# conv_ffn: taps, silu and gate product on the products in PSUM, and GpSimd's share of the weight splits by a running sum

## The chip, the cores and the metric

One Trainium2 chip; the kernel runs on one of its cores. The metric is the device time of one execution in microseconds, the median of several runs. TensorE (PE) makes the matrix products into PSUM; VectorE (DVE), ScalarE (ACT) and GpSimd (POOL) work on tiles; SyncE (SP) issues the loads.

## The reference, cut to what matters

Two blocks of two layers each, all in float32, on 256 latent tokens and 256 context tokens of width 1024. The change bears on the feed-forward part at the end of each layer of the second block. It makes 2 x 2816 features of each token, convolves them over the tokens (the latents stand on a grid of 4 rows of 64 and get 3 x 3 taps; the context gets three taps along its row), and gates one half with the other:

```python
def conv_ffn(h, w_up, conv_w, conv_b, w_down, rows):
    u = h @ w_up
    if rows is None:
        u = dwconv1d(u, conv_w[1], conv_b)
    else:
        u = dwconv2d_grid(u, conv_w, conv_b, rows)
    a, g = jnp.split(u, 2, axis=-1)
    return (jax.nn.silu(g) * a) @ w_down
```

Layer 0 does this for latents and context, layer 1 for the latents alone.

## The kernel before

Every float32 product is made of three float32r products: each operand is the sum of a high and a low part, and `mm3` adds high times high, high times low and low times high. A weight is loaded into a `raw` tile (three of them, 1 MB each, `load`), and `wsplit` (line 413) makes `wh` on ACT, a copy of `raw`, and `wl`, the difference of `raw` and `wh`. That difference is made on DVE, or on GpSimd when the running number of splits is a multiple of `lo_pool`. `lo_pool` is set by stage: 4 or 5 in the first block and in the first mixer of the second, 2 in `conv_ffn` of layer 0, 3 in the mixer of layer 1, 1 in `conv_ffn` of layer 1, where GpSimd so makes every low half.

`conv_ffn` (line 1590) walks over 22 feature tiles of 128, two to a load. An iteration makes two products, of a tile of `a` and the tile of `g` that gates it (`q` 0 and 1), transposed: features on partitions, tokens along the row, 512 of them in layer 0 (`ns` 2: latents, then context) and 256 in layer 1. A product is eight times `mm3`, 24 matmuls. It lands in a PSUM tile of the tag `mm`, of which there are two. ACT reads it twice: `o` (tag `fo`, four tiles) is the middle tap with the bias, `u` (tag `fu`, three tiles) a copy in SBUF. The taps are then DVE instructions `o = u * w + o` (`stt`, line 187): eight for the latents, over 189, 192 or 252 of the 256 tokens, since the edges of the grid are left out, and in layer 0 two for the context, over 255. After both products of an iteration ACT takes silu of the second `o`, DVE multiplies the two `o`, ACT copies the result into the high half of `G` (named `cg` in the trace) and DVE subtracts to make the low half.

The down product (`dense_out`) uses `G` as its stationary operand, with three PSUM tiles `acc` and one `gv`; the two tiles of the tag `aux` serve transposes before and after `conv_ffn`. In layer 0 it runs after each of two parts (12 and 10 feature tiles). In layer 1 a group of its products, four feature tiles by both halves of the columns, is put after the feature tiles 8, 12, 16 and 20, a group behind, and the rest at the end. A scheduler at build time sets the order of each engine's queue from the dependences and the free tiles; on the chip each engine takes its queue in order.

Of the kernel before, what the change touches and what calls it, by code (L numbers as in the profile page):

```python
# [18 lines left out]
T = 256  # L19
# [10 lines left out]
# in each sub-block, the tiles of 128 columns to a step of the conditions' products  # L30
PACE = (6, 6.5, 8, 7, 7.5, 6.5)
# and the splits of weights to one whose low part is made by GpSimd
LO_POOL = (4, 4, 4, 4, 4, 5)
# the parts of the context's projections at the end of each sub-block of the first block
# [8 lines left out]
def _consts():  # L43
# [24 lines left out]
    # in both float32 and float32r  # L68
# [11 lines left out]
    # one-hot of the bucket of each distance j - 127  # L80
# [5 lines left out]
    # reversed, so that row p, column s reads p + s  # L86
# [8 lines left out]
    # name, reshape rows of 128  # L95
# [13 lines left out]
class _Pair:  # L109
    """hi and lo parts of a float32 tensor, each exact in float32r."""  # L110
# [11 lines left out]
class _K:  # L122
    def __init__(self, ctx, tc, I, out, dbg=None):
# [9 lines left out]
        self.nsplit = 0  # L133
# [9 lines left out]
    def fill(self, units):  # L143
        """one more step of the work for the gaps after each so many tiles of a matrix product"""
        self.credit += units
        while self.credit >= self.pace:
            self.credit -= self.pace
            next(self.filler, None)
# [5 lines left out]
    def weave(self, *gens):  # L154
        """traces (generator, steps) side by side, each at its share"""
        gens = [[g, n, 0] for g, n in gens]
        while gens:
            x = min(gens, key=lambda x: (x[2] + 0.5) / x[1])
            x[2] += 1
            try:  # L160
                next(x[0])
            except StopIteration:
                gens.remove(x)
# [34 lines left out]
    def silu2(self, out, p, th):  # L198
        """out = 2 silu(p); th: space for tanh"""
# [21 lines left out]
    def rows(self, pool, src, n, tag, bufs=1):  # L221
        """a vector of n in DRAM, the same in each partition"""
# [32 lines left out]
    def more_setup(self, pool):  # L255
        """what is wanted after the first products"""
# [17 lines left out]
    def all_mods(self):  # L274
        second = self.second_mods()
        for k in self.mods:
            if k == (1, 0):
                # the first norm's of the context are wanted early
# [6 lines left out]
    def vectors(self, b0, b1, raw, engs, loads=None):  # L285
        """vectors with the index along partitions: blocks b0 to b1 of 128 columns; raw [128, blocks, 128]"""
# [23 lines left out]
    def gemv(self, w, c0, conds):  # L310
        """partial sums [128, 512] of conds @ w[:, c0:c0+512], to be summed over partitions"""
# [15 lines left out]
    def gemv_cols(self, w, c0, conds, bias, outs, plus=0.0):  # L327
        """outs [128, 8]: cond @ w[:, c0:c0+1024] + bias + plus, by feature"""
# [10 lines left out]
    def start_loads(self):  # L339
        """the weights of the first modulation and the first rows"""  # L340
# [13 lines left out]
    def start_mod(self, A, B):  # L354
        """the first modulation, a part of it on the tensor engine"""
# [18 lines left out]
    def gemv_rows(self, w, c0, conds, bias, out, scale=1.0, plus=0.0):  # L374
        """out [conds, 1024] in DRAM: scale * (cond @ w[:, c0:c0+1024] + bias + plus); bias by feature"""
        n = len(conds)
        for h in range(2):
# [15 lines left out]
            # its product comes when its operand is there  # L393
# [19 lines left out]
    def wsplit(self, r):  # L413
        """[128, a, n], at most 1024 in a partition -> (hi, lo)"""
# [5 lines left out]
        self.nsplit += 1  # L420
        eng = self.nc.gpsimd if self.nsplit % self.lo_pool == 0 else None
# [3 lines left out]
    def mm3(self, out, stat, mov, start, stop):  # L425
        """out += stat.T @ mov, both (hi, lo)"""
# [7 lines left out]
    def prod_T(self, p, W, hT, ks=range(KT)):  # L434
        """p [n, T] = (h @ w).T for n columns of w"""
# [3 lines left out]
    def dense_T(self, hT, w, c0, n, evac, prep=None):  # L439
        """(h @ w[:, c0:c0+n]).T, evac(feature tile, psum [128, tokens])"""  # L440
# [11 lines left out]
    def dense_rows(self, hT, w, c0, n, evac, prep=None):  # L452
        """h @ w[:, c0:c0+n], evac(column, width, token tile, psum [128, width])"""
# [17 lines left out]
    def dense_out(self, stat, nk, w, evac, nt=2, both=False, tag="acc"):  # L471
        """g @ w with w [nk * 128, 1024]; stat(k): g.T's tile k as (hi, lo) [128, tokens]; evac(half, token tile,
        psum [128, 512]); both: the halves of the columns side by side up to the last tiles, else one after the other"""
        # the last ones' products are long, for what waits for the first tokens' results
# [27 lines left out]
    def to_T(self, n, A, B, hT, full=None):  # L502
        """n [128, 2, 1024] by tokens -> (n * A + B).T as a pair [128, 8, 256], and whole in full; A, B [128, 8]"""
# [25 lines left out]
    def ffn(self, hT, w_in, w_out, post, tail, more):  # L529
        """tail: what follows the last product; more: further work beside the first; both with room in the given pool"""  # L530
# [21 lines left out]
    def post_ln(self, i, x, Grow):  # L552
        """x: rows in DRAM; (evac of a dense_out, finish): LN(alpha x + G y) -> normalized rows, rows in DRAM"""
# [41 lines left out]
    def first_mod(self, l, j):  # L595
        """A = g (1 + scale), B = b (1 + scale) + shift, with the norm g, b before"""
# [13 lines left out]
    def first_block(self, n):  # L610
        """its first n sub-blocks"""
# [6 lines left out]
    def operand(self, i, hT=None):  # L618
        """the modulated rows ahead of sub-block i, by feature"""
# [3 lines left out]
    def sub_block(self, i, hT, nxt, before=None):  # L623
        """nxt: whether the next one's operand follows here; before: more to do ahead of the last product"""
# [16 lines left out]
        def tail(pool):  # L641
# [3 lines left out]
            # what the context's mLSTM needs, where the next products wait for the norm  # L645
# [22 lines left out]
    def mix_setup(self):  # L668
        nc, I = self.nc, self.I
        # rel_bias by distance: [128 queries, head, 256 keys], query 128 + q  # L670
# [21 lines left out]
    def lower_bound(self):  # L692
        nc, I = self.nc, self.I
        # 1 - lower bound of the second layer: softmax over layers, summed, less the first
# [47 lines left out]
    def merge(self, l, gp, YH, YL, sgd, post, more):  # L742
# [5 lines left out]
        for b in range(4):  # L748
# [6 lines left out]
            for i in range(2):  # L755
# [8 lines left out]
                # twice the sum; the half is in the gate  # L764
# [1172 lines left out]
```

## Time and profile before

| | |
|---|---|
| time, median of three runs | 3027.41 us (3025.47 to 3045.25) |
| span of the profiled execution | 3027.7 us |
| PE, DVE, ACT, POOL busy in the span | 89%, 80%, 44%, 28% |
| low halves made on GpSimd, on DVE | 233, 432 |
| taps of `conv_ffn` (DVE) | 792 |
| granted TensorE clock, mean | 0.948 |

The profile is that of one execution, which took as long as the median run. [...] "Idle before" is the time that an engine stood still ahead of a group of instructions, with what ended it. [...] The feed-forward part of layer 0 lies between about 1941 and 2318 us of the span, with two stretches of taps, and that of layer 1 between about 2720 and 3018 us.

### The profile page before, as it was taken

What the parts mean: (1) busy time and instruction counts of PE and PEld (TensorE: products, weight loads), DVE (VectorE), ACT (ScalarE), POOL (GpSimd) and SP (SyncE); (2) the same over time, 40 slices, a digit from 0 to 9 for tenths busy, and PEclk for the clock granted to TensorE, in tenths of its full rate; (3) what the DMA queues carried; (4) which work ended last, traced back from release to release, by engine and by line L of the source; (5) the groups of instructions that cost most, each with busy time, mean ns of one, the idle gap of its engine ahead of it and who ended that gap; (6) DMA issues with size and microseconds to landing.
All of it is one profiled execution on the core that took longest, in us unless ns stands there. A gap on an engine that the chain in (4) does not pass through costs nothing. (4 is left out here: it accounts for less than half of the span.)

```text
span 3027.7 us, 44224 instructions
## 1 busy us (share of the span) xinstructions
PE 2703.0 (89%) x16988; PEld 2398.9 (79%) x16988; DVE 2429.3 (80%) x3939; ACT 1337.1 (44%) x2171; POOL 834.3 (28%) x462
## 2 busy tenths in 40 slices
PE   7998998899899899989998998899988989886776
PEld 7987898799799788879987887777877767666665
DVE  7777898877888988797657767798596678879987
ACT  3444444444454444444445453543243534434433
POOL 1123121322321412232112212222222122425665
PEclk9998999899999999989999999999999999988888
DMA  9897677788798775678672141422322322233332
GB/s 317 277 316 245 216 231 245 225 293 273 237 310 287 227 243 185 207 235 298 228 217 85 32 143 51 162 84 98 98 74 90 89 67 71 83 111 99 112 112 97
DMA packets 406300, 534.78 MB, mean 177 GB/s; under 512 B 25061, under 2 KB 279881, under 8 KB 404553
## 3 DMA queue, kind: packets, MB, share of 16 engines
q1 hardware_dynamic: 404357, 531.22, 53.6%
q8 instruction: 133, 2.18, 0.3%
q10 hardware_dynamic: 1732, 0.74, 0.1%
q14 instruction: 78, 0.64, 0.1%
HBM read 515.61 MB, written 16.31 MB: 176 GB/s over the span
## 5 line engine op out<-in xcount | busy, mean ns | idle before, releaser
L175 POOL TENSOR_TENSOR wl<-raw,wh 128x1024 fp32r<-128x1024 f32 x233 | 619.0, 2662 | 1651.2 <-ACT wh L196 1472.9
L196 ACT ACTIVATE wh<-raw 128x1024 fp32r<-128x1024 f32 x665 | 696.1, 1053 | 761.5 <-PE mm L169 374.9
L169 PE MATMUL mm<-hTh,wh 128*128 128x256 f32 (+1 forms) x2552 | 805.6, 316 | 77.9 <-ACT fu L196 73.5
L169 PE MATMUL mm<-hTh,wl 128*128 128x256 f32 (+1 forms) x2552 | 791.6, 310 | 10.1 <-DVE wl L175 5.5
L169 PE MATMUL mm<-hTl,wh 128*128 128x256 f32 (+1 forms) x2552 | 793.1, 311 | 3.3 <-DVE hTl L175 3.3
L175 DVE TENSOR_TENSOR wl<-raw,wh 128x1024 fp32r<-128x1024 f32 (+1 forms) x432 | 537.0, 1247 | 193.2 <-ACT wh L196 190.6
L169 PEld LDWEIGHTS mm<-hTh,wh 128*128 128x128 f32 x2552 | 496.8, 195 | 115.7 <-ACT fu L196 83.8
L169 PEld LDWEIGHTS mm<-hTh,wl 128*128 128x128 f32 x2552 | 495.4, 194 | 34.6 <-DVE wl L175 6.4
L169 PEld LDWEIGHTS mm<-hTl,wh 128*128 128x128 f32 x2552 | 496.8, 195 | 27.4 <-DVE hTl L175 4.0
L187 DVE SCALAR_TENSOR_TENSOR fo<-fu,colv,fo 128x189 f32<-128x189 f32 (+3 forms) x792 | 468.0, 632 | 32.6 <-ACT fu L196 22.6
L187 DVE SCALAR_TENSOR_TENSOR acc<-graw,cond,acc 128x512 f32<-128x512 f32 x504 | 465.6, 939 | 23.6 <-ACT acc L196 9.6
L169 PE MATMUL acc<-wl,gh 128*128 128x512 f32 x352 | 139.4, 396 | 0.9 <-DVE wl L175 0.9
L169 PE MATMUL acc<-wh,cg 128*128 128x512 f32 x396 | 138.7, 409 | 1.6 <-ACT wh L196 1.6
L169 PE MATMUL acc<-wh,gh 128*128 128x512 f32 x352 | 140.0, 398 | 0.0
L169 PE MATMUL acc<-wh,gl 128*128 128x512 f32 x352 | 139.3, 396 | 0.0
L169 PE MATMUL mm<-hlh,wl 128*128 128x256 f32 (+1 forms) x456 | 130.9, 287 | 1.5 <-POOL wl L175 1.1
L169 PE MATMUL mm<-hll,wh 128*128 128x256 f32 (+1 forms) x456 | 130.4, 286 | 1.1 <-DVE hll L175 1.1
L169 PE MATMUL mm<-hlh,wh 128*128 128x256 f32 (+1 forms) x456 | 130.8, 287 | 0.3 <-DVE g L175 0.2
L169 PE MATMUL mm<-wh,hTh 128*128 128x256 f32 x384 | 114.3, 298 | 8.3 <-DVE hqT L187 3.6
L169 PE MATMUL mm<-wh,hTl 128*128 128x256 f32 x384 | 110.7, 291 | 2.5 <-DVE hTl L175 2.4
L169 PE MATMUL mm<-wl,hTh 128*128 128x256 f32 x384 | 111.4, 291 | 0.0
L196 ACT ACTIVATE fo<-fo 128x512 f32<-128x512 f32 (+1 forms) x44 | 23.1, 525 | 198.6 <-DVE fo L187 198.5
(546 smaller groups left out, 5142.7 us busy)
## 6 DMA issues: line engine op xcount, KB each, us to landing
raw<-in_ffn_w_in_dram SPq DMA_DIRECT2D x88, 1024.0 KB
graw<-in_w_ada_dram SPq DMA_DIRECT2D x128, 512.0 KB
raw<-in_mix_w_in_dram SPq DMA_DIRECT2D x52, 1024.0 KB
graw<-in_mod_w_dram SPq DMA_DIRECT2D x96, 512.0 KB
raw<-in_ffn_w_up_dram SPq DMA_DIRECT2D x44, 1024.0 KB
raw<-in_ffn_w_out_dram SPq DMA_DIRECT2D x40, 1024.0 KB
raw<-in_even_w_in_dram SPq DMA_DIRECT2D x28, 1024.0 KB
raw<-in_ffn_w_down_dram SPq DMA_DIRECT2D x20, 1024.0 KB
```

Of the source, the lines that this page charges most:

```text
L169: self.nc.tensor.matmul(out, lhsT, rhs, start=start, stop=stop)
L175: (eng or self.nc.vector).tensor_tensor(out=out, in0=a, in1=b, op=op)
L187: self.nc.vector.scalar_tensor_tensor(out, a, s, b, op0=op0, op1=op1, **kw)
L196: self.nc.scalar.activation(out, a, f, **kw)
```

## The change

Three edits, two of them in `conv_ffn`.

The copy `u` in SBUF is gone. The product's PSUM tile is itself `u`; it comes from the tags `mm` and `aux` in turn, two tiles each, so that products of `a` take one pair of banks and products of `g` the other. The taps read `u` there. Silu, which wrote over the second `o`, writes into the `u` of the second product, the gate product is written over it in PSUM, and the split of `G` reads it from there.

`wsplit` adds `1 / lo_pool` to a running sum and gives the split to GpSimd when the sum reaches one, which is then taken off. `lo_pool` can so be a fraction, and in `conv_ffn` of layer 1 it becomes 1.15. The other stages keep their numbers.

Comments and docstrings are dropped throughout the file; those lines of the diff are left out here.

```diff
-        self.nsplit += 1
-        eng = self.nc.gpsimd if self.nsplit % self.lo_pool == 0 else None
+        self.nsplit += 1 / self.lo_pool
+        eng = None
+        if self.nsplit >= 1:
+            self.nsplit -= 1
+            eng = self.nc.gpsimd
...
             parts = ((0, FT),) if ns == 1 else ((0, 12), (12, FT))
+            tags = cycle(("mm", "aux"))
             for j0, j1 in parts:
...
                         for q, raw in enumerate(rs):
-                            p = self.ps([128, ns * T])
+                            u = self.ps([128, ns * T], next(tags))
                             W = raw[:, :, i * 128:(i + 1) * 128]
-                            self.prod_T(p, self.wsplit(W), hT)
+                            self.prod_T(u, self.wsplit(W), hT)
                             ch = q * FT + j + i
-                            u = fp.tile([128, ns * T], F32, tag="fu", name="fu", bufs=3)
                             o = fp.tile([128, ns * T], F32, tag="fo", name="fo", bufs=4)
                             out.append(o)
-                            self.act(o, p, AF.Identity, scale=cw(1, 1, ch), bias=self.col("ffn_conv_b_2", layer * 44 + ch))
-                            self.act(u, p)
+                            self.act(o, u, AF.Identity, scale=cw(1, 1, ch), bias=self.col("ffn_conv_b_2", layer * 44 + ch))
...
-                        self.act(out[1], out[1], AF.Silu)
-                        self.mul(out[0], out[0], out[1])
+                        self.act(u, out[1], AF.Silu)
+                        self.mul(u, out[0], u)
                         g = fp.tile([128, 2, ns * T], F32R, tag="G", name="cg", bufs=j1 - j0 if ns == 1 else 12)
-                        self.split(g[:, 0], g[:, 1], out[0])
+                        self.split(g[:, 0], g[:, 1], u)
...
-        self.lo_pool = 1
+        self.lo_pool = 1.15
         ss = self.conv_ffn(1, ss)
```

## Rows read from the trace of the kernel before

**Rows 1.** By stretch: window, length, PE PEld DVE ACT POOL busy, clock, DMA, GB/s.
```profile
1948.30:2110.00 161.70, 148.07 (x630) 118.60 (x629) 151.90 (x276) 68.27 (x99) 34.94 (x13) 0.99 0.26 85
2160.00:2299.80 139.80, 128.49 (x551) 102.40 (x549) 129.49 (x232) 56.67 (x82) 30.10 (x12) 1.00 0.25 83
2727.90:3001.20 273.30, 196.22 (x1215) 178.31 (x1214) 256.02 (x396) 108.11 (x192) 168.09 (x58) 0.87 0.34 110
...
2979.70:3017.00 37.30, 29.60 (x116) 22.98 (x115) 26.41 (x39) 13.97 (x23) 25.89 (x9) 0.91 0.18 57
```

**Rows 2.** Groups by shape, layer 1: shapes, count | busy us, mean ns | idle before.
```profile
L175 POOL TENSOR_TENSOR wl<-raw,wh 128x1024 fp32r<-128x1024 f32 x68 | 192.6, 2852 | 132.5 <-ACT wh L196 132.5
L187 DVE SCALAR_TENSOR_TENSOR fo<-fu,colv,fo 128x189 f32<-128x189 f32 x176 | 128.4, 752 | 13.2 <-ACT fu L196 12.4
L169 PE MATMUL mm<-hTh,wh 128*128 128x256 f32 x352 | 108.2, 308 | 49.2 <-ACT fu L196 49.0
...
L187 DVE SCALAR_TENSOR_TENSOR fo<-fu,colv,fo 128x192 f32<-128x192 f32 x88 | 74.5, 863 | 0.5
...
L187 DVE SCALAR_TENSOR_TENSOR fo<-fu,colv,fo 128x252 f32<-128x252 f32 x88 | 50.1, 569 | 1.0
...
L169 PE MATMUL acc<-wl,cg 128*128 128x512 f32 x66 | 30.4, 460 | 24.2 <-POOL wl L175 24.2
...
L196 ACT ACTIVATE fo<-fo 128x256 f32<-128x256 f32 x22 | 9.2, 417 | 67.5 <-DVE fo L187 67.4
```

**Rows 3.** Groups by shape, layer 0 (1940 to 2310 us).
```profile
L169 PE MATMUL mm<-hTh,wh 128*128 128x512 f32 x352 | 140.3, 399 | 24.5 <-ACT fu L196 24.5
...
L187 DVE SCALAR_TENSOR_TENSOR fo<-fu,colv,fo 128x192 f32<-128x192 f32 x88 | 79.1, 899 | 1.5
L187 DVE SCALAR_TENSOR_TENSOR fo<-fu,colv,fo 128x189 f32<-128x189 f32 x176 | 74.3, 424 | 3.2
...
L187 DVE SCALAR_TENSOR_TENSOR fo<-fu,colv,fo 128x252 f32<-128x252 f32 x88 | 42.3, 481 | 3.0
...
L196 ACT ACTIVATE fu<-mm 128x512 f32<-128x512 f32 x44 | 26.0, 591 | 0.0
...
L175 DVE TENSOR_TENSOR fo<-fo 128x512 f32<-128x512 f32 x22 | 15.2, 692 | 5.0 <-ACT fo L196 4.3
```

**Rows 4.** Timelines of POOL and DVE around 2158 us: start, length, instruction, [idle before].
```profile
2158.09 2.42 POOL L175 TENSOR_TENSOR wl<-raw,wh 128x1024 fp32r<-128x1024 f32 x1 [13.00 <-ACT wh L196]
...
2158.35 0.69 DVE L175 TENSOR_TENSOR tof<-gv,Gc 128x512 f32<-128x512 f32 x1 [1.38 <-PE gv L169]
2159.07 1.98 DVE L175 TENSOR_TENSOR rc<-rc,tof 128x512 f32<-128x512 f32 x1
2160.97 1.22 DVE L175 TENSOR_TENSOR wl<-raw,wh 128x1024 fp32r<-128x1024 f32 x1
```

**Rows 5.** Groups by shape, whole span: DVE with a PSUM operand.
```profile
L175 DVE TENSOR_TENSOR tof<-acc,G 128x512 f32<-128x512 f32 x42 | 28.6, 686 | 41.6 <-PE acc L169 38.8 <-DMA G<-gates 2.8
...
L193 DVE TENSOR_SCALAR tof<-aux,mod 128x256 f32<-128x256 f32 x24 | 12.5, 542 | 6.8 <-ACT tof L196 6.1
...
L187 DVE SCALAR_TENSOR_TENSOR oz<-g,mm 128x256 f32<-128x256 f32 x16 | 6.7, 418 | 7.0 <-ACT g L196 7.0
```

**Rows 6.** The chain that ended last: start, length, what.
```profile
2690.04 10.03 PE acc L169 x43
...
2722.28 4.65 PE mm L169 x33
...
2836.89 4.96 PE mm L169 x43
```

**Rows 7.** Groups of ACT in layer 0's second part, up to its seventh silu.
```profile
L196 ACT ACTIVATE wh<-raw 128x1024 fp32r<-128x1024 f32 x16 | 16.9, 1055 | 14.2 <-PE mm L169 10.4 <-issue 3.3 <-PE gv L169 0.4
...
L196 ACT ACTIVATE fo<-fo 128x512 f32<-128x512 f32 x7 | 4.4, 632 | 41.5 <-DVE fo L187 41.5
```

**Rows 8.** Timeline of ACT in layer 1.
```profile
2849.68 1.06 ACT L196 ACTIVATE wh<-raw 128x1024 fp32r<-128x1024 f32 x1 [4.48 <-DMA raw<-in_ffn_w_up_dram]
```

More of the change, by code (lines that the diff above doesn't have):

```diff
@@ L2 @@
 from contextlib import ExitStack
-from itertools import chain, islice
+from itertools import chain, cycle, islice
 import numpy as np
@@ L132, in __init__ @@
         self.gp = None
-        self.nsplit = 0
+        self.nsplit = 0.0
         self.lo_pool = 4
```

## Prediction

> **What bounds the kernel now.** I read the page first: over the whole span PE is the busiest engine, but a share of the span names no bound, and the change bears on two stretches, the two calls of `conv_ffn`. So next came the table by stretch. [...] In both, DVE is nearly full and PE pauses.
>
> Third, the groups by shape show what fills DVE. A tap over 189 elements takes 424 ns on average in layer 0 and 752 in layer 1; taps of 192 elements, three more, take 899 and 863 [rows 2, 3]. That is no price by the element: some taps are long. The timeline shows which. While GpSimd makes the low half of a weight (2.42 us from 2158.09), DVE's product of a PSUM tile with SBUF rows takes 0.69, as always; the next instruction, an add of two SBUF tiles, takes 1.98 and ends as GpSimd does, where a product of two SBUF tiles of that size takes 0.69 on average [rows 3, 4]. I read from it that a DVE instruction with both tensors in SBUF stands still while GpSimd's runs, and one with a tensor in PSUM does not. In layer 1 GpSimd makes every low half, so nearly each catches a tap.
>
> What it costs PE is the idle time ahead of its products, put down to the copy `fu`: 24.5 us in layer 0, 49.0 in layer 1 [rows 2, 3]. The copy is not slow (0.59 us in layer 0): it stands in ACT's queue behind a silu that waits for taps, 67.4 us in layer 1 [rows 2, 3], and it needs one of three `fu` tiles that the taps free.
>
> **The change part by part.** *The copies.* 88 ACT passes go, 44 x 591 ns = 26 us of them in layer 0 [rows 3]. ACT is under half busy in all three stretches [rows 1], so I cost this at nothing in itself.
>
> *The taps, the gate product and its split* each get one tensor in PSUM. What blocking takes today, by the free price of 424 and 481 ns: layer 1, 176 x (752 - 424) + 88 x (863 - 424) + 88 x (569 - 481) ns = 57.7 + 38.6 + 7.7 = 104 us; layer 0, 88 x (899 - 424) = 42 us [rows 2, 3].
>
> Does a tensor in PSUM cost more by itself? The nearest rows: the taps' own instruction over 256 elements with a PSUM tensor takes 418 ns, less than the free 424 for 189 elements in SBUF; products of 512 elements out of PSUM average 686 over the whole run, GpSimd's work included, against 692 for SBUF alone [rows 3, 5]. I take 0, which is the lower end too, since the rows differ by 6 ns. The upper end is a two-scalar operation out of PSUM, 542 ns for 256 elements, 0.12 us more; it is another instruction, and 418 is the nearer row [rows 5]. [...]
>
> *Layer 1's new pace.* DVE without blocking: (256.0 - 104) / 22 = 6.9 us an iteration (two products, their taps, a gate product). GpSimd's share falls from all to 1/1.15: of 66 splits about 9 go to DVE, 9 x 1.22 = 11 us, and these still have both tensors in SBUF, so each can lose up to one GpSimd operation, 9 x 2.4 = 22 us [rows 4]. That gives 7.4 to 8.4; I take 7.7. PE at full clock: a matmul of 256 columns each 4.96 / 43 = 0.115 us, of 512 each 10.03 / 43 = 0.233 [rows 6]. An iteration is 48 of the first, 5.5 us; each of the four groups of the down product between iterations is 48 of the second, 11.2 us; all of layer 1 is 1056 x 0.115 + 264 x 0.233 = 183 us.
>
> The first ten iterations have no down product: DVE is their bound, 77 us. Of the other twelve, with three groups, PE is, 12 x 5.5 + 3 x 11.2 = 100 us, plus what it still waits for GpSimd's halves. The down product waits 24.2 us for them now; with 0.87 of them on GpSimd and each 2.42 instead of 2.85 us, three quarters, 18 us, stay [rows 2, 4]. So 77 + 118 = 195 us from 2722.3 [rows 6] to the last product's end, now at 2979.7 [rows 1], 257 us: -62. The tail after it (37.3 us, a down group and the last 72 matmuls [rows 1]) I leave. Bounds: -40 (8.4 us in the first ten, and the others keep a third more of their idle) and -107 (PE's 183 us and 5 for the last taps, instead of 295).
>
> *Layer 0's new pace.* DVE: (281.4 - 42) / 22 = 10.9 us an iteration; PE 48 x 0.233 = 11.2. So PE becomes the bound, and its 24.5 us of idle are all there is to win. DVE, 97% as loaded as PE, will still make it wait at times. I take three quarters, -18, between 0 and -24.5.
>
> *The banks.* Today two banks hold a product only until two ACT reads are done, of which the copy takes 0.59 us [rows 3]. Now a bank is held to its last tap, the gate's to the split, and four banks hold two iterations. ACT's order today: up to the seventh silu of layer 0's second part it has made sixteen high halves, products 0 to 15, and that silu needs 12 and 13 [rows 7]: two products ahead, which four banks still allow. In layer 0 the gate's bank is free about 3 x 0.63 + 4.5 + 2 x 0.69 = 7.8 us after its product: three ACT passes (middle tap, silu, high half) [rows 7], ten taps, product and low half [rows 3]. PE wants it three products later, 3 x 5.6 = 16.8 us. I cost the banks at 0; if the cover goes, it is the last but one rival.
>
> *The running sum elsewhere.* GpSimd's share stays one in `lo_pool`; only which one can shift, where `lo_pool` changes. A split costs 2.42 on GpSimd or 1.22 on DVE [rows 4]; a few shifted ones are within 3 us either way, and I take 0.
>
> **Sum.** 3027.7 - 62 - 18 = 2948 us against the profiled span; the median, 3027.41, differs by 0.01%, so it is the time too.
>
> **The rivals.** *PE's floor:* the waits vanish, -107 - 24.5, 2896. For it: layer 0's PE holds clock 1.00 where it is fed [rows 1]. Against: every low half on GpSimd still takes 2.4 us ahead of its matmuls.
>
> *The weights become the bound:* half of layer 1's gain and half of layer 0's go, 2988. For it: in layer 1 a high half waits 4.48 us for its load [rows 8]. Against: with three raw tiles, each 4.5 us to load, 1.06 and 2.85 to split, held for two more splits, six splits a round of three tiles, 6s = 8.4 + 2s gives a pace s of 2.1 us a split, below PE's 2.8 (24 x 0.115).
>
> [...]
>
> *Slower, ACT's queue:* with banks held longer the built order may put the next gate's high half behind silu and split, so that one product is made ahead instead of two. In layer 0 an iteration is then those 7.8 us less the low half, 7.1, plus 1.06 and 2.42 for the weight [rows 4, 8], 10.6, and a product of 5.6: 16.2 against 13.7, +55. In layer 1, 0.42 + 3.5 + 3 x 0.42 + 1.06 + 2.42 + 2.8 = 11.5 against 273.3 / 22 = 12.4, -20. Together 3063. It turns the sign once layer 0's loop passes 13.7 by more than the 0.9 us that layer 1's wins. Against: rows 7, where two are ahead.
>
> *No gain:* what blocks moves to other work, 3020 or so. Against: nothing else in either stretch pairs two SBUF tensors in such number.
>
> **Chances and range.** Forecast (2920 to 2975) 0.55; floor (below 2920) 0.17; weights 0.13; dear PSUM taps 0.06; ACT's queue 0.05; no gain 0.04. About 1% either way, 2997 to 3058, is what a measurement of this kernel can tell from no change. Faster is 0.55 + 0.17 + 0.13 + a third of the PSUM case, 0.87; same 0.08; slower 0.05. The range goes from the floor, 2895, to 2992, past weights and PSUM taps; left out are the last two cases, part of the dear taps and a bit at each end, 2 in 10.
>
> **What would show it.** Right: taps of 189, 192 and 252 elements near 424 and 481 ns in both layers, none near 2.4 us; GpSimd's operation near 2.4 instead of 2.85 in layer 1; no `fu`; layer 1 from first product to last gate split some 205 us instead of 280, at a clock above 0.87; layer 0's parts 9 us shorter each. Wrong: taps that are all longer (PSUM is dear); PE idle put down to a DVE split or ACT's high half (banks, queue); high halves that wait for `raw` longer than 4.5 us again and again (weights); or work before 1940 us that moves by more than 3 us.

## The result, and the profile after

The changed kernel takes 2956.94 us (median of four runs, 2942.87 to 2964.8) against 3028.76 us of the kernel before (median of four): 71.8 us less by the medians. The ratio of the runs on record is 0.9743, interval 0.9705 to 0.9781, which would be 78 us. The prediction was 2948 us, with a range of 2895 to 2992. Where gains are given "by the ratios" below, they are such ratios times 3030 us. The profiled execution has a span of 2949.0 us.

Taps first, since the argument rests on them. In the list of instructions by tile of the changed kernel (engine, operation and count; shortest/median/longest ns), for products in either pair of banks:

```profile
L187 DVE SCALAR_TENSOR_TENSOR fo<-mm,colv,fo x396: 394/410/483, 1965.2 to 2915.4; 128x189 f32<-128x189 f32 x88, 128x252 f32<-128x252 f32 x44, 128x192 f32<-128x192 f32 x44, 128x255 f32<-128x255 f32 x22
L187 DVE SCALAR_TENSOR_TENSOR fo<-aux,colv,fo x396: 394/414/484, 1970.2 to 2919.2; 128x189 f32<-128x189 f32 x88, 128x252 f32<-128x252 f32 x44, 128x192 f32<-128x192 f32 x44, 128x255 f32<-128x255 f32 x22
```

Of 792 taps none takes longer than 484 ns, with GpSimd at work beside them. In the kernel before the means alone went up to 899 ns [rows 2, 3].

The table by stretch answers [rows 1] (window, length, busy of PE, PEld, DVE, ACT, POOL, granted clock, DMA share, GB/s): layer 0's two parts and layer 1 from the first centre tap to the last split; layer 1 to the last instruction of a computing engine; the tail from the last product's end. Busy time is the union of an engine's instructions, and the granted clock is TensorE's, as a share of its full speed. Matmuls overlap: in the kernel before, between 2837 and 2842 us at clock 1.00, each over 256 columns lasts 0.28 us and the next starts 0.118 us after it.

```profile
1964.00:2102.80 138.80, 138.80 (x607) 113.66 (x606) 120.94 (x277) 57.12 (x75) 30.09 (x13) 1.00 0.30 99
2162.90:2282.00 119.10, 119.10 (x512) 96.45 (x511) 102.24 (x231) 46.85 (x62) 25.25 (x11) 1.00 0.29 93
2710.60:2922.80 212.20, 181.63 (x1209) 167.42 (x1208) 153.21 (x404) 96.44 (x148) 123.31 (x51) 0.93 0.43 142
...
2710.60:2945.80 235.20, 197.96 (x1278) 180.24 (x1276) 164.49 (x423) 103.58 (x160) 132.40 (x56) 0.93 0.40 133
2911.40:2949.00 37.60, 26.39 (x111) 20.34 (x109) 18.71 (x37) 12.97 (x21) 16.39 (x8) 0.94 0.22 76
```

In layer 0 PE is busy for the whole of both parts, at clock 1.00: the stage is at PE's floor. In layer 1 no engine is full: DVE has gone from 94% of the stretch up to the last split to 72%, PE's clock from 0.87 to 0.93. The groups by shape in layer 1 show what is left (shapes, count | busy us, mean ns | idle before), to be held against [rows 2]:

```profile
L175 POOL TENSOR_TENSOR wl<-raw,wh 128x1024 fp32r<-128x1024 f32 x54 | 131.3, 2435 | 99.9 <-ACT wh L196 99.8
...
L169 PE MATMUL aux<-hTh,wh 128*128 128x256 f32 x170 | 52.1, 306 | 18.4 <-DVE cg L175 18.4
...
L187 DVE SCALAR_TENSOR_TENSOR fo<-aux,colv,fo 128x189 f32<-128x189 f32 x88 | 35.8, 407 | 15.8 <-ACT fo L196 15.3
...
L169 PE MATMUL acc<-wl,cg 128*128 128x512 f32 x66 | 26.7, 405 | 1.5 <-POOL wl L175 0.9 <-DVE wl L175 0.6
...
L187 DVE SCALAR_TENSOR_TENSOR fo<-mm,colv,fo 128x192 f32<-128x192 f32 x44 | 18.0, 409 | 0.2
...
L175 DVE TENSOR_TENSOR wl<-raw,wh 128x1024 fp32r<-128x1024 f32 x9 | 11.7, 1301 | 10.8 <-ACT wh L196 10.8
```

The 49.0 us that PE waited for the copy are gone, and of the 24.2 us that the down product waited for GpSimd 0.9 stay. A new wait stands in their place: 18.4 us for `cg`, DVE's low half of the gate product, which is the last reader of the gate's bank. GpSimd's own operation went from 2.85 to 2.44 us.

To find the time I cut each profile at four events: the first centre tap of layer 0, its last split, the first centre tap of layer 1 and the last instruction of a computing engine.

| us | before | after | difference | predicted |
|---|---|---|---|---|
| start to first tap of layer 0 | 1948.3 | 1964.0 | +15.7 | 0 |
| layer 0, to its last split | 351.7 | 318.0 | -33.7 | -18 |
| to the first tap of layer 1 | 428.0 | 428.6 | +0.6 | 0 |
| layer 1, to the end | 296.6 | 235.2 | -61.4 | -62 |

So the sum was met while two of its terms were off by about 16 us each, in opposite directions; that they cancel is luck. The experiments take the change apart.

### The profile page after: what moved, and what is told of

Its sections match the earlier page's. It is cut to its first block, busy times and chain, and to the rows that moved or that the text cites. A ratio compares the mean times of both kernels' runs of the same rounds, so it can differ in the third digit from the quotient of the medians.

```text
span 2949.0 us, 44177 instructions
## 1 busy us (share of the span) xinstructions
PE 2673.3 (91%) x16988; PEld 2377.6 (81%) x16988; DVE 2267.2 (77%) x3949; ACT 1305.5 (44%) x2083; POOL 774.6 (26%) x452
## 5 line engine op out<-in xcount | busy, mean ns | idle before, releaser
L169 PE MATMUL mm<-hTh,wh 128*128 128x256 f32 (+2 forms) x2200 | 680.2, 310 | 6.9 <-DVE g L175 3.6
L169 PE MATMUL mm<-hTh,wl 128*128 128x256 f32 (+2 forms) x2200 | 669.4, 305 | 10.0 <-DVE wl L175 9.9
L169 PE MATMUL mm<-hTl,wh 128*128 128x256 f32 (+2 forms) x2200 | 669.9, 305 | 3.1 <-DVE hTl L175 3.1
L169 PEld LDWEIGHTS mm<-hTh,wh 128*128 128x128 f32 (+1 forms) x2200 | 426.1, 194 | 27.0 <-issue 4.2
L169 PEld LDWEIGHTS mm<-hTh,wl 128*128 128x128 f32 (+1 forms) x2200 | 425.0, 193 | 27.5 <-DVE wl L175 11.8
L169 PEld LDWEIGHTS mm<-hTl,wh 128*128 128x128 f32 (+1 forms) x2200 | 425.8, 194 | 20.4 <-DVE hTl L175 3.5
L187 DVE SCALAR_TENSOR_TENSOR fo<-aux,colv,fo 128x189 f32<-128x189 f32 (+3 forms) x396 | 170.1, 430 | 20.3 <-ACT fo L196 17.1
L187 DVE SCALAR_TENSOR_TENSOR fo<-mm,colv,fo 128x189 f32<-128x189 f32 (+3 forms) x396 | 169.9, 430 | 16.5 <-ACT fo L196 13.6
L169 PE MATMUL aux<-hTh,wh 128*128 128x512 f32 (+1 forms) x352 | 123.3, 350 | 18.4 <-DVE cg L175 18.4
L169 PE MATMUL aux<-hTh,wl 128*128 128x512 f32 (+1 forms) x352 | 122.2, 347 | 4.8 <-DVE wl L175 4.8
```

Of the source, the lines that this page charges most:

```text
L169: self.nc.tensor.matmul(out, lhsT, rhs, start=start, stop=stop)
L187: self.nc.vector.scalar_tensor_tensor(out, a, s, b, op0=op0, op1=op1, **kw)
```

## Experiments

**1. The products in PSUM alone.** The changed kernel, with the share of GpSimd by the old modulus and 1 in layer 1.

```diff
-        self.nsplit += 1 / self.lo_pool
-        eng = None
-        if self.nsplit >= 1:
-            self.nsplit -= 1
-            eng = self.nc.gpsimd
+        self.nsplit += 1
+        eng = self.nc.gpsimd if self.nsplit % self.lo_pool == 0 else None
...
-        self.lo_pool = 1.15
+        self.lo_pool = 1
```

> The PSUM edit alone: every n-th split to GpSimd by the running number as before, and every one in layer 1. Blocking theory (a DVE instruction with two SBUF tensors stands still while GpSimd works): nearly the whole gain, layer 1 from first product to the end 240 to 255 us (before 307, after 244), layer 0 from first to last product as after, some 313 us; no tap over 0.6 us. The first 1940 us tell whether the running sum cost the 14 to 16 us by which the changed kernel reached layer 0 later: if so this kernel reaches it within 4 us of the kernel before, and its time is 2930 to 2945; if that is scatter between executions, about 2957. Rival (the share made the gain): above 3000.

Measured: 2915.18 us, 0.9614 of before [0.9594, 0.9634], some 39 us better than the whole change by the two ratios, and better than the 2930 to 2945 that I had expected at best. Layer 0 takes 318.8 us, as in the whole change (318.0); layer 1 takes 208.3. Its window in the table by stretch:

```profile
2701.10:2909.40 208.30, 187.50 (x1278) 170.67 (x1276) 153.95 (x414) 102.92 (x160) 151.57 (x65) 0.99 0.45 150
```

Against the changed kernel's 235.2 us, PE is busy 10.5 us less (clock 0.99 for 0.93) and idle 20.8 instead of 37.2. The wait for the gate's bank is 8.0 us. PSUM is all of the gain, and the share takes some of it back.

**2. The share alone.** The kernel before with the running sum and 1.15 (the same edit of `wsplit` as in the change).

> The running sum and 1.15 alone, taps on SBUF copies as before. Blocking theory: taps are still caught; in layer 1 about 50 instead of 58 of them, 8 x 2.1 = 17 us less on DVE against 9 x 1.22 = 11 us more for the low halves it makes itself: layer 1 within 15 us of before. If the running sum costs time elsewhere, 3035 to 3045; if not, 3015 to 3030. Rival (the share made the gain): below 2980.

Measured: 3050.12 us, 1.0059 [1.0044, 1.0075], so 18 us slower, a little above the 3035 to 3045 that I had expected if the sum costs time elsewhere. In layer 1 it wins 5.4 us (291.2). The groups by shape there, DVE:

```profile
L187 DVE SCALAR_TENSOR_TENSOR fo<-fu,colv,fo 128x189 f32<-128x189 f32 x176 | 121.1, 713 | 8.3 <-ACT fu L196 7.5
L187 DVE SCALAR_TENSOR_TENSOR fo<-fu,colv,fo 128x192 f32<-128x192 f32 x88 | 59.9, 698 | 0.4
```

The taps are still caught: with 57 low halves on GpSimd instead of 66 there is hardly less to be caught by. The loss lies ahead of layer 0, whose first tap comes at 1971.7 us (experiment 5).

**3. PSUM for the sums, copies kept.** The changed kernel, but ACT still copies each product to SBUF for the taps to read, and the running sum of the taps stands in PSUM instead.

```diff
-    u = self.ps([128, ns * T], next(tags))
-    self.prod_T(u, self.wsplit(W), hT)
-    o = fp.tile([128, ns * T], F32, tag="fo", name="fo", bufs=4)
-    self.act(o, u, AF.Identity, scale=cw(1, 1, ch), bias=...)
+    o = self.ps([128, ns * T], next(tags))
+    self.prod_T(o, self.wsplit(W), hT)
+    u = fp.tile([128, ns * T], F32, tag="fu", name="fu", bufs=3)
+    self.act(u, o)
+    self.act(o, o, AF.Identity, scale=cw(1, 1, ch), bias=...)
...
-    self.mul(u, out[0], u)
+    self.mul(out[1], out[0], u)
+    u = out[1]
```

> The 88 copies into SBUF are back, but the accumulator stays in PSUM in place of the product, so that each tap still has one tensor in each. Share and four banks as after. Blocking theory: as after within 20 us, 2940 to 2975, no tap over 0.6 us, though ACT works 42 us more. Rival (ACT relieved of the copies made the gain): 3000 to 3030. The rival that four banks made it expects 2957 here too; the next kernel tells that.

Measured: 2960.5 us, 0.975 [0.9723, 0.9777], that is the time of the change; layers 318.0 and 230.3 us. The taps in layer 1, group by shape:

```profile
L187 DVE SCALAR_TENSOR_TENSOR mm<-fu,colv,mm 128x189 f32<-128x189 f32 x88 | 36.5, 415 | 26.7 <-ACT mm L196 26.3
```

and the longest of PE's waits there (us in total, times, longest):

```profile
PE mm L169 <- DVE aux L175: 23.7, 10, 5.1
```

One tensor in PSUM is enough, whichever of the two it is (415 ns here for taps of 189 elements, 406 and 407 in the change). The copies that ACT no longer makes are worth nothing; a bank is again what PE waits for (23.7 us in 10 waits), here that of `a`, which DVE's gate product reads last.

**4. Four banks alone.** The kernel before, its products in `mm` and `aux` in turn, copies kept.

```diff
-    p = self.ps([128, ns * T])
+    p = self.ps([128, ns * T], next(tags))
```

> The kernel before with products in four banks in turn; copies, taps in SBUF and share as before. Blocking theory: the taps are caught as before and DVE stays the bound, 3015 to 3040. Rival (four banks let PE run ahead and made the gain): 2950 to 2980.

Measured: 3034.27 us, 0.9999 [0.9981, 1.0017]; layers 350.0 and 296.6 us. The taps of layer 1, group by shape:

```profile
L187 DVE SCALAR_TENSOR_TENSOR fo<-fu,colv,fo 128x189 f32<-128x189 f32 x176 | 127.7, 752 | 13.2 <-ACT fu L196 12.4
L187 DVE SCALAR_TENSOR_TENSOR fo<-fu,colv,fo 128x192 f32<-128x192 f32 x88 | 76.6, 885 | 0.5
```

and PE's waits there:

```profile
PE acc L169 <- POOL wl L175: 23.9, 5, 5.8
PE aux L169 <- POOL wl L175: 15.4, 9, 2.1
PE mm L169 <- POOL wl L175: 14.0, 4, 5.7
```

PE's wait has another name, GpSimd's low half and for 25.3 us ACT's high half instead of the copy, and the stage is as long as it was: while DVE is held up, more room ahead of it buys nothing.

**5. The share, one piece at a time.** Three kernels on the products in PSUM. The first keeps the running sum and has 1 in layer 1:

```diff
-        self.lo_pool = 1.15
+        self.lo_pool = 1
```

> The changed kernel with a share of one in layer 1 instead of 1/1.15; the running sum stays. In layer 1 from the first o to the end the PSUM edit alone took 208 us, the changed kernel 235. If it is the nine low halves on DVE that cost it, this one takes 205 to 215 there and 2922 to 2938 in all; the rest to the 2915 of the PSUM edit alone is then the running sum in the stages before. If it is the running sum's other choices, it stays at 230 to 240 and at about 2957.

The second is experiment 1 with a sum of 1/1.15 in layer 1 alone, which gives nine low halves to DVE:

```diff
+        if self.share is not None:
+            self.share += 1 / 1.15
+            eng = None
+            if self.share >= 1:
+                self.share -= 1
+                eng = self.nc.gpsimd
...
-        self.lo_pool = 1
+        self.share = 0.6
```

> The PSUM edit with the share by the running number everywhere except in layer 1, where 1/1.15 by a sum puts the same nine splits on DVE as the changed kernel. If those nine cost the 27 us in layer 1: 230 to 240 us there and 2935 to 2947 in all; what is then missing to 2957 is the running sum's choices before layer 0. If they cost nothing: 2910 to 2920.

The third is experiment 1 with `lo_pool` 2 in layer 1, which gives 33 to DVE.

> The PSUM edit alone, but in layer 1 only every second low half on GpSimd, 33 on DVE. If a low half on DVE costs by waiting in its queue behind taps (27 us for 9), layer 1 gets worse with their number: 33 give 240 to 300 us from the first o to the end, 2945 or more in all. If only the place of those nine is bad, or relief of GpSimd is worth something, 195 to 225 us, at most 2932.

Measured, with the first experiment and the change for comparison:

| share | low halves of layer 1 on DVE | us | ratio to before | first tap of layer 0 | layer 1 |
|---|---|---|---|---|---|
| modulus (experiment 1) | 0 | 2915.18 | 0.9614 [0.9594, 0.9634] | 1954.5 | 208.3 |
| sum | 0 | 2927.78 | 0.9656 [0.9630, 0.9682] | 1965.9 | 208.8 |
| modulus | 9 | 2935.12 | 0.9674 [0.9647, 0.9700] | 1949.9 | 229.6 |
| sum (the change) | 9 | 2956.94 | 0.9743 [0.9705, 0.9781] | 1964.0 | 235.2 |
| modulus | 33 | 2957.16 | 0.9746 [0.9718, 0.9773] | 1957.2 | 249.3 |

Both halves of the edit cost, and mainly in different places. The nine halves on DVE cost 21.3 us in layer 1 (208.3 to 229.6), 33 cost 41.0. (The change itself takes 235.2 us there with the same number: PE is busy 4.4 us more, at clock 0.93 for 0.95, and idle 1.2 us more; what lowered the clock is open.) DVE has the time, as the window of the second kernel shows:

```profile
2698.90:2928.50 229.60, 193.58 (x1278) 175.90 (x1276) 164.52 (x423) 103.72 (x160) 132.33 (x56) 0.95 0.41 136
```

DVE's 10.6 us more still leave it idle for 65 us. But PE is busy 6.1 us more at a lower clock and idle 15.2 us more: a low half on DVE stands in line with the taps. In the change the one at 2783.61 us starts behind thirteen taps, at least 5.1 us after its high half was done, and PE waits 4.85 us for it. DVE also waits for ACT's high half, as the changed kernel's group above has it (10.8 us in two waits, of 6.7 and 4.0), but these held little up: after the first the next tap's `o` had been there for 0.8 us when the low half ended, and after the second DVE waited another 1.94 us for the next `o`. PE's wait for the gate's bank is 8.0 us in experiment 1 and 8.7 in the first kernel here, both without the nine, and 18.4 with them in the change, and PE now waits for the low halves themselves too, in the change

```profile
PE aux L169 <- DVE wl L175: 4.8, 1, 4.8
PE mm L169 <- DVE wl L175: 3.0, 2, 2.3
```

In the third kernel PE's waits in that stretch say the same:

```profile
PE aux L169 <- DVE wl L175: 19.7, 5, 4.6
PE aux L169 <- DVE cg L175: 15.9, 8, 2.5
```

The running sum costs ahead of layer 0. The first tap of layer 0 comes at 1946.1 to 1957.9 us in the nine profiles in which GpSimd's turns before it go by the modulus, mean 1951.9, and at 1964.0, 1965.9, 1971.7 and 1979.2 in the four that go by the sum, mean 1970.2. Up to about the 330th split the two rules pick the same splits, and the mean times at which its high half starts differ by 4.1 us, which the choice of splits does not explain. By the 430th, past three changes of `lo_pool` at which the sum picks others, they differ by 20.4. Which of these splits does it was not looked for. In layer 1, where both give every split to GpSimd, the two rules are alike (208.3, 208.8).

**6. GpSimd silent.** Is a tensor in PSUM worth something by itself, or only against GpSimd? The kernel before, and experiment 1, each with no low half of `conv_ffn` on GpSimd: DVE makes all 132, of which 99 were GpSimd's.

```diff
-        self.lo_pool = 2
+        self.lo_pool = 10000
         ss = self.conv_ffn(0, ss, xc)
...
-        self.lo_pool = 1
+        self.lo_pool = 10000
         ss = self.conv_ffn(1, ss)
```

The kernel before:

> The kernel before (copies, taps in SBUF), but in both calls of conv_ffn every low half is made by DVE and none by GpSimd. It takes away what the blocking theory blames and adds work to the engine it says is full. Blocking theory: no tap over 0.6 us; layer 0 then has 33 x 1.22 = 40 us more on DVE and 42 us less of blocking, layer 1 66 x 1.22 = 81 us more and 104 less: both layers within 15 us of before or a little faster, together 0 to -30, 3000 to 3033. Rival (long taps are DVE's own, whatever GpSimd does): DVE is full and gets 121 us more, 3100 to 3150.

The kernel of experiment 1:

> The changed taps (products read in PSUM, four banks, no copies) with the share by the modulus and no low half of either conv_ffn layer on GpSimd: all 132 go to VectorE. Beside it stands the earlier run of the kernel before with the same no-GpSimd edit (2963.3 us; 254.6 us from the first centre tap of layer 1 to the end, taps 409 to 475 ns out of SBUF). Theory (the change is worth what it frees VectorE of GpSimd, nothing else): with GpSimd silent the products in PSUM bring nothing more, layer 0 stays at some 306 us and layer 1 at 245 to 265, so 2953 to 2973 us. Rival (reading PSUM, or the copies that ScalarE no longer makes, is worth something by itself): layer 1 at 240 or less and under 2945 us. A second rival (banks held to the end of the split while VectorE also makes each weight's low half): layer 1 at 270 or more, over 2975.

Measured: 2963.29 us, 0.976 [0.9731, 0.9789], with everything in SBUF, and 2979.48 us, 0.9813 [0.9789, 0.9838], with the products in PSUM. The first result I had badly underrated: with two numbers changed in two lines it is as good as the whole change. Its windows, layer 0's two parts and layer 1, have

```profile
1956.60:2096.70 140.10, 140.10 (x602) 113.56 (x601) 135.09 (x289) 69.15 (x99) 0.00 (x0) 1.00 0.30 97
2157.90:2275.70 117.80, 117.80 (x515) 96.47 (x514) 113.70 (x241) 56.57 (x82) 0.00 (x0) 1.00 0.28 92
2703.80:2958.40 254.60, 201.38 (x1278) 184.12 (x1276) 221.20 (x477) 118.08 (x204) 1.09 (x2) 0.88 0.37 122
```

and its taps in SBUF, group by shape in layer 1, are

```profile
L187 DVE SCALAR_TENSOR_TENSOR fo<-fu,colv,fo 128x189 f32<-128x189 f32 x176 | 68.3, 409 | 0.5
```

In layer 0 that is PE's floor as well (319.1 us). In this window of layer 1 DVE makes 63 low halves more than before and is busy 221.2 us instead of 268.1: what GpSimd took off DVE there, 63 x 1.22 = 77 us, was less than what it held DVE up. With the products in PSUM and GpSimd silent, layer 1 takes 255.7 us, no less, and layer 0 331.8, 13 more. The total is past the 2953 to 2973 of my theory; of the second rival, that the banks cost, layer 0 shows a part and the time of layer 1 nothing. (This profile is of the fastest of the four runs, 2968.84 us; the two ratios' intervals just touch.) The waits of PE in layer 1:

```profile
PE aux L169 <- DVE cg L175: 20.0, 8, 4.0
PE aux L169 <- DVE wl L175: 15.4, 4, 4.7
```

So a tap out of PSUM is neither dearer nor cheaper (407 ns, and 409 out of SBUF). Its whole worth is that GpSimd's help then hardly holds DVE up: with GpSimd 2915 us in PSUM and about 3030 in SBUF, without it 2979 and 2963. In layer 0, where PE is never idle with everything in SBUF, it is now idle for 6.6 us, 3.7 of it for the gate's bank and 2.4 for low halves on DVE: there the banks' cost shows, since nothing else is gained.

**7. The gate's bank.** Experiment 1, with the gate product written over the first `o` in SBUF, so that the bank is free at the product, before the split.

```diff
-        self.mul(u, out[0], u)
+        self.mul(out[0], out[0], u)
...
-        self.split(g[:, 0], g[:, 1], u)
+        self.split(g[:, 0], g[:, 1], out[0])
```

> The version with products in PSUM and the share by the modulus at 1 in layer 1 (2915.2 us), but the gate product is written to the value's tile in SBUF, so that the gate's bank comes free at the product and not at the end of its split. Theory (the bank held through the split is TensorE's last wait on VectorE in layer 1: 8.0 us of 208): that wait goes to under 3 us, layer 1 comes to 198 to 206, some 2905 to 2912 us. Rival (the split's subtraction now has both operands in SBUF and stands still while GpSimd works, as all taps did before): the subtraction grows from 421 ns to 700 to 1000 in the mean, 6 to 13 us more of VectorE over 22 products, the gate's wait goes but the accumulators' chain is later: 2912 to 2925 us.

Measured: 2916.46 us, 0.9612 [0.9587, 0.9638], no different from experiment 1; layer 1 takes 210.0 us. The low half of the gate product in layer 1, group by shape:

```profile
L175 DVE TENSOR_TENSOR cg<-fo,cg 128x256 fp32r<-128x256 f32 x22 | 38.3, 1740 | 8.0 <-ACT cg L196 8.0
```

and PE's waits:

```profile
PE aux L169 <- DVE fo L175: 8.3, 6, 2.3
PE mm L169 <- DVE fo L187: 4.4, 6, 1.4
```

In experiment 1 that subtraction has an operand in PSUM:

```profile
L175 DVE TENSOR_TENSOR cg<-aux,cg 128x256 fp32r<-128x256 f32 x22 | 9.3, 421 | 8.3 <-ACT cg L196 8.3
```

With both in SBUF it takes 1740 ns instead of 421, 29 us more in all and well over the 700 to 1000 that I had expected. The bank comes free one step earlier of a DVE that runs later, and PE waits as long. It is the mechanism of this case in one instruction. How much one group is held up depends on what else can be: in the kernel before, where the taps stood in GpSimd's way as well, the same subtraction took 616 ns in the mean, and 419 with GpSimd silent (experiment 6).

**8. More raw tiles.** Experiment 1 with six tiles for raw weights in layer 1 instead of three.

```diff
-        raw = self.wraw.tile([128, 2048], F32, tag="raw", name="raw")
+        raw = next(self.raws)()
...
+            if ns == 1:
+                self.raws = cycle([lambda: self.wraw.tile(..., name="raw"),
+                                   lambda: fp.tile(..., name="raw", bufs=3)])
```

> The version with products in PSUM and the share by the modulus at 1 in layer 1 (2915.2 us), with six tiles for raw weights in layer 1 in place of three. In its layer 1 TensorE is busy 187.5 of 208.3 us, ScalarE's splits wait 6.6 us for the loads of raw weights and the load queue waits for GpSimd 199 us (its splits are the last readers of a raw tile). Theory (the loads are now among the last things TensorE waits for in layer 1): the waits of splits for loads fall under 2 us and layer 1 to 195 to 204 us: 2903 to 2911. Rival (GpSimd's 2.4 us for each split, 141 of 208 us, and the banks set the pace, loads come in the shade of them): layer 1 stays at 205 to 211 us, 2911 to 2920.

Measured: 2907.62 us, 0.9592 [0.9570, 0.9613], an interval that overlaps that of experiment 1. Layer 1 takes 207.1 us against 208.3, and this profile's lead of 8.7 us at the end is there, to 0.3 us, before layer 0 begins. The total falls into my theory's range and layer 1 into the rival's, and layer 1 is what the edit touches. The waits of ACT's splits for loads are gone from the list of waits, and PE's stay (6.8 us for the gate's bank, 3.1 for high halves): the loads were hidden. The weights are not the bound.

**9. GpSimd elsewhere.** If its help costs more than it gives in `conv_ffn` before the change, what does it do in the rest of the kernel, where taps are not the point? Experiment 1 with GpSimd's low halves in the two `conv_ffn` layers alone.

```diff
-LO_POOL = (4, 4, 4, 4, 4, 5)
+LO_POOL = (10000,) * 6
...
-        self.lo_pool = 2 if l else 4
+        self.lo_pool = 10000
...
-        self.lo_pool = 3
+        self.lo_pool = 10000
         ss = self.odd()
```

(the initial 4 and the 5 of one more stage likewise. As the diff has it, `lo_pool` was 2 in one stretch of the first block too, not 4 or 5 throughout.)

> The version with products in PSUM and the share by the modulus (2915.2 us; first centre tap of layer 0 at 1954.5 us, last split of layer 0 to first centre tap of layer 1 428 us), but GpSimd makes low halves only in the two conv_ffn layers: some 115 before layer 0 and some 60 between the layers go to VectorE. It asks whether what holds in the conv_ffn layers of the kernel before (GpSimd's help costs VectorE more than it saves) holds where most of the kernel runs. There each such split costs VectorE about 1.22 us, 140 us before layer 0 with VectorE busy 1540 of 1954; against it, the 504 accumulations of the conditions' products take 943 ns where the free price of 512 elements is about 690, 127 us in all. Theory (the two balance): first centre tap of layer 0 at 1940 to 1970 us, in all 2900 to 2940. Rival (TensorE waits there for each low half in turn, and a queue of VectorE that is fuller delivers them later, whatever the busy time): 30 to 100 us more, 2945 to 3015. Second rival (GpSimd's help costs more than it saves everywhere): under 2895.

Measured: 2840.44 us, 0.9359 [0.9344, 0.9375], the fastest of all and 77 us below experiment 1 by the ratios. I had put my theory on a balance; the second rival held. The first tap of layer 0 comes at 1905.5 us instead of 1954.5, the stretch between the layers 409.2 us instead of 427.8 (GpSimd had made 19 low halves there, not the 60 of the expectation); the layers themselves are unchanged (318.8 and 207.9). The groups of DVE ahead of layer 0, of this kernel:

```profile
L175 DVE TENSOR_TENSOR wl<-raw,wh 128x1024 fp32r<-128x1024 f32 x474 | 583.0, 1233 | 161.1 <-ACT wh L196 158.6
L187 DVE SCALAR_TENSOR_TENSOR acc<-graw,cond,acc 128x512 f32<-128x512 f32 x504 | 379.7, 769 | 13.2 <-ACT acc L196 5.5 <-DMA graw<-in_mod_w_dram 5.0 <-DMA graw<-in_w_ada_dram 0.3
```

and of experiment 1:

```profile
L187 DVE SCALAR_TENSOR_TENSOR acc<-graw,cond,acc 128x512 f32<-128x512 f32 x504 | 467.8, 943 | 22.8 <-ACT acc L196 10.4 <-DMA graw<-in_w_ada_dram 5.9 <-DMA graw<-in_mod_w_dram 2.8
L175 DVE TENSOR_TENSOR wl<-raw,wh 128x1024 fp32r<-128x1024 f32 x360 | 450.2, 1254 | 147.5 <-ACT wh L196 145.9 <-PE mm L169 0.2
```

DVE makes 114 low halves more, 133 us of work, and 88 us come back from one group alone, 504 accumulations that go from 943 to 769 ns; all in all DVE is busy 1523 us up to the first tap instead of 1540, and PE is idle 137 us instead of 166 and busy 20 us less at clock 0.97 for 0.95. It was not GpSimd's slower halves that PE waited for: in experiment 1 that comes to some 3 us of the stretch. The stages outside `conv_ffn`, which I had left alone as none of the change's business, held another 77 us beside the 117 of experiment 1.

## Why the prediction was right, and where it was not

**Blocked taps: right.** That DVE stands still while GpSimd works when both its tensors are in SBUF, and not with one in PSUM, was read from four lines of a timeline [rows 4]. One reading there was loose: the add of that timeline does not end as GpSimd does but 0.54 us after it, about the 0.69 that it takes when free, as an instruction would that starts when GpSimd is done. In the trace of the kernel before, 53 of the 352 taps of layer 1 take over 0.6 us, 2.46 in the mean, and 55 of GpSimd's 58 operations up to the last split overlap one. Experiments 1, 3, 6 and 7 bear it out, each from another side. One subtraction takes 421 ns with an operand in PSUM and 1740 with both in SBUF (experiments 1 and 7); one operand in PSUM for the taps, the gate product and its split is worth some 117 us of 3030 (experiment 1).

**PSUM costs nothing by itself: right.** 407 ns for taps of 189 elements in layer 1, with GpSimd at work or silent, against a free 409 out of SBUF (experiment 6). That taps out of PSUM are dear, 0.06 of the chances, no run shows. Copies into SBUF did not pay while GpSimd worked: experiment 3 keeps them and is no faster. With GpSimd silent the kernel with copies came out ahead, 0.976 against 0.9813 (experiment 6), in layer 0 and not in its taps.

**The copies: right** at nothing (experiment 3).

**Layer 0, -18: too small; the step that failed is the term of PE's idle.** (The 281.4 us of DVE in the prediction are the two parts of [rows 1] added up, and an iteration of 13.7 us, against which ACT's queue is held, is their 301.5 us / 22.) I kept a quarter of the 24.5 us of idle, and none stayed. And I counted idle alone. In the first part PE's busy time for the same matmuls fell by 3.9 us, at clock 1.00 instead of 0.99 (129.2 to 125.3 us up to its last product). And the stretch ends at DVE's last split, which came 18.8 us after PE's last product and comes 13.5 after it: 5.3 us. The three make up the 33.7 measured. The same lag at the end of the first part is no term of its own, since PE is busy for the 73.5 us from its last product there to the first tap of the second part, before as after (73.6).

**Layer 1, -62: right in sum, wrong in its parts.** The product stage went from 258.8 to 206.8 us, where I had 195, and the tail, which I left as it was, from 48.1 us to the span's end to 37.6. The two errors cancel, which is luck again. In the tail PE's idle ahead of its last matmul went from 7.7 to 1.3 us and its busy time from 30.8 to 26.4, with ten matmuls fewer behind the last product (111 for 121) and at clock 1.00 instead of 0.91. The waits of PE from 2979.7 us on in the kernel before have

```profile
PE acc L169 <- POOL wl L175: 7.4, 2, 5.7
```

so 7.4 of the 24.2 us that I had placed in the stage stood in the tail. DVE's last split, too, came 21.5 us after PE's last product and comes 11.4 after it; that this is what brought GpSimd's halves forward is not shown.

In the stage, the ten iterations or so ahead of the first down group took 72.8 us (77 predicted), and the rest 134.0 (118). The failing term is there, and it is above all the nine low halves of the next paragraph: without them (experiment 1) the rest takes 113.9. I also costed the banks at nothing, worked out for layer 0 alone, where it held with GpSimd at work; in layer 1 an iteration of PE is half as long, and PE waited 18.4 us for the gate's bank, 8.0 without the nine.

**Nine low halves to DVE: right in sign, far too small.** I charged DVE 0.8 us in each of the first ten iterations, 8 us, and credited the rest with some 3, as GpSimd's share shrank: 5 us in all. Measured, they cost 21 us of layer 1 (experiment 5), 5.2 of them ahead of the first down group (68.4 to 73.6) and 15.0 in the rest (113.9 to 128.9), where I had a credit. The charge went by DVE's busy time and by GpSimd holding these nine up, which it hardly did: they take 1301 ns each, and 1221 with GpSimd silent (experiment 6). What it left out is the queue. In the trace of the change 3388 of DVE's instructions, 1956 of ACT's and 428 of GpSimd's come, by line and tile, in the order in which they were built, so a low half is made when the work ahead of it is done: the one at 2783.61 us kept PE waiting for 4.85 us (experiment 5). That the nine also delay the splits that free a bank is my estimate from PE's longer wait there, 18.4 us for 8.0; no run moved them to another place in the queue. Without them (experiment 1) the stage is 182.3 us: 68.4 ahead of the first down group, close to the 6.9 us of DVE an iteration that I had worked out, and 113.9 for the rest, where I had put PE's floor at 100. Products in PSUM alone, at 2915 us, so come nearer to the rival of PE's floor, 2896, than to the forecast.

**The running sum, 0 within 3 us: wrong.** Ahead of layer 0 it cost 18.3 us in the mean of the profiles, 11.4 and 14.1 in the two pairs of experiment 5. I had looked at how many splits shift and not at which work stands behind them; that the same number of turns (116 before layer 0 under either rule) in another order can move the time by half a per cent I did not think of. Which work it is stays open.

Of the rivals, the weights fall with experiment 8, dear taps with the tap rows, and ACT's queue with layer 0, where PE never waits. No gain is refuted by the total. Of the prediction's signs of being right, the taps, GpSimd's operation, the copy and the clock came as said; layer 1 from its first product to its last gate split took 218.2 us instead of 280.3, not some 205. Two of its signs of being wrong are met, PE idle put down to a DVE split (18.4 us) and work before 1940 us that moves by more than 3 us, and both pointed at the right culprits.

## What to carry to other kernels

Before giving VectorE's work to GpSimd, look for VectorE instructions whose mean is above their shortest: the difference times their count, over all groups, against the time of what GpSimd takes over, says whether the help is one. Ahead of layer 0 133 us of work moved back, 88 us came back in one group, and over all groups VectorE was busy 17 us less. As a forecast of the time this test was too cautious both times: by it I expected a balance, and 0 to 30 us, where the kernel won 77 and 73 (experiments 9 and 6), as TensorE's idle and busy time fell with it. Where GpSimd's help is wanted, put one operand of the VectorE instructions beside it into PSUM (421 ns for 1740 in the subtraction of experiment 7), and cost the bank that this holds in the stage with the shortest iteration (TensorE waited 8.0 us for it in experiment 1 and 18.4 in the change). Before moving an instruction into the queue of an engine that has time to spare, cost what stands ahead of it there and what behind it (4.85 us of TensorE's wait for one low half, experiment 5). When idle time behind a slow engine is counted, count also how far that engine ends behind the others at the end of the stretch.

## What the runs showed of the hardware that was not expected

A subtraction of 421 ns took 1740 on average when both its operands were in SBUF (experiments 1 and 7; GpSimd is busy for 152 of the 208 us of that stage in experiment 1): a short instruction waited out 1.3 of GpSimd's 2.4 us in the mean. And GpSimd loses too: its low half of 128x1024 took 2852 ns beside taps in SBUF [rows 2] and 2435 beside taps in PSUM.

PE's granted clock in layer 1 rose as its pauses went: 0.87 with 85 us of idle before, 0.93 with 37 in the change, 0.95 with 36 in the second kernel of experiment 5, 0.99 with 21 in experiment 1; not by their sum alone, since experiment 7 has 0.97 with 20. The means are made of two levels: in the kernel before the clock is 0.50 between 2747 and 2749 us, where matmuls over 256 columns start 0.213 us apart, and 1.00 between 2837 and 2842 us, where they start 0.118 apart. In experiment 1 against the change a shorter stage came by 10.5 us from fewer busy microseconds for the same matmuls and by 16.4 from less idle.
